# Norms of q and k through a 0/1 matrix, row-wise block transposes, and another rank for the local part

## The chip, the cores and the metric

The kernel runs on one core of one Trainium2 chip. The metric is device time in microseconds (us) of one execution; lower is better. An instruction belongs to one engine and each engine runs its own list in order: TensorE (PE) multiplies matrices, VectorE (DVE) and ScalarE (ACT) do elementwise work, GpSimd (POOL) does some of it too, and SyncE (SP) only issues DMA transfers. An instruction that waits for another engine or a transfer holds up everything behind it in its own list.

## The reference

One layer of a hybrid encoder, for a prompt of 2048 tokens and a sample of 32 tokens with a carried state:

```python
h = rmsnorm(x) * (1 + sc1) + sh1
p = h @ w_in                        # columns for u, v, q, k, vv, z, a, b
u, v = split(gelu(p_uv)); v = rmsnorm(v)
a_out = u * (W_s v + b_s)           # spatial gating over 128 positions
q, k, vv = silu(causal_conv(qkv))   # width 4
q = q * rsqrt(sum(q*q) + EPS) * 128 ** -0.5      # per token and head
k = k * rsqrt(sum(k*k) + EPS)
o, S = gated_delta_rule(q, k, vv, beta, g, S0)   # chunked, 4 heads of 128
b_out = rmsnorm(o) * silu(z)
x = x + gate1 * (concat(a_out, b_out) @ w_out)
h = rmsnorm(x) * (1 + sc2) + sh2
x = x + gate2 * (relu(h @ w_up) ** 2 @ w_down)
y = rmsnorm(x)
```

What matters here is the squared norm of every token's q and k in each head (a sum over 128 channels), and the transposed k and v, with tokens as rows, that the delta rule reads.

## The kernel before

Activations lie with channels on the 128 partitions and tokens along the row. Fp32 products of the large GEMMs are made from a high and a low half of each operand: `BH`/`BL` are the halves of the activations, `wh`/`wl` those of a weight slab. ACT writes the high half (a copy into a rounding type), DVE the low half (a subtraction); this is the "split" of a slab or of an activation, and a slab is split in two parts of 1024 columns. The program goes in stages: a startup (conditioning, z columns), the mixers in two halves of 1024 and 1056 tokens (the second with the sample), the output projection, the feed-forward part in three blocks of tokens.

In a half, `qkv_tile` makes one tile of q, k or v of one head, in two or three groups of 512, 384 or 288 tokens: 24 matmuls into a PSUM bank `g`, eviction by ACT into `raw`, the convolution by ACT and three DVE operations into `y`, SiLU into the row `yo`. Then one DVE instruction (`transpose32`) transposes the 32 x 32 blocks of `yo` into `yt`; k and v go from there to DRAM (`kt_d`) in four transfers. For k and q the tile `yt` is squared in place and summed over the 32 channels that each row now holds (`sums`, into `part`), and the four partial sums per token go to DRAM (`ns_d`).

`delta_local` is the delta rule's part that has no recurrence: it loads the decays (`dm`), loads the partial norms back, transposes them by a PE product with the identity (bank `B`), adds up the four parts, takes the reciprocal root, and then, for each of four batches of two chunks of 128 tokens, loads q and k from DRAM (`kq_d` into the ring `kq1`), multiplies k by (k, q) into bank `L` and evicts this by DVE. `delta_inv` inverts the triangular blocks of a pair of heads, a ladder of small PE products in bank `B` with DVE steps between them (block transposes `tr()` among them). `delta_chain` is the recurrence over chunks (bank `C`), `delta_out` its output, and `sample` all of this for the 32 sample tokens.

No order is written by hand. Every helper records an operation with an engine, an estimated cost and one of the ranks `CHAIN, INV, LOCAL, EVAC, GEMM, IDLE` (0 to 5). `schedule` then plays through the program with the estimated costs: at each moment the engine that is free takes the ready operation with the smallest key, and the order so found is the order of the instructions. Large GEMM products have rank GEMM, the local part LOCAL, and everything with no rank of its own EVAC: evictions, the splits, the convolution, the transposes, and the DMA loads for them. DMA issues are ordered in the same way, in the one queue of SP. A PE product that becomes ready early is thus fitted between GEMM products; how long things really take changes nothing in the order.

Of the kernel before, what the change touches and what calls it, by code (L numbers as in the profile page):

```python
# [17 lines left out]
P = 128  # L18
# [10 lines left out]
T0 = [0, 1024]  # L29
TW = [1024, 1056]  # L30
CHUNKS = [list(range(0, 8)), list(range(8, 17))]
WZ = 260
# [167 lines left out]
def R(x):  # L200
    return x.ap if isinstance(x, View) else x
# [11 lines left out]
class Program:  # L213
# [40 lines left out]
    def schedule(self):  # L254
# [91 lines left out]
class Kern:  # L346
# [57 lines left out]
    def transpose32(self, out, in_):  # L404
        nc = self.nc
        self.p.op(DVE, 68 + 1.042 * out.n, lambda: nc.vector.transpose(R(out), R(in_)), [out], [in_])

# [151 lines left out]
    def setup(self):  # L559
# [30 lines left out]
        rg("sp", [(6, 0)], (P, 3, 256))  # L590
        rg("ssl", [(6, 512), (6, 640)], (P, P))
# [39 lines left out]
        for n, s in (("convw", (P, 12, 4)), ("sconv", (P, 12, 3)), ("halo", (P, 12, 3)), ("cvo", (P, 2, 12, 3)),  # L631
                     ("ab", (P, 2, NC_, H)), ("ssv", (P, 2, NC_)), ("rq", (P, H, NC_)), ("ck", (P, H, NC_)),
                     ("dngc", (P, 1)), ("dtb", (P, H)), ("alog", (P, H)), ("nea", (P, H)), ("cs", (P, KT, 2)),
                     ("craw", (P, KT, 2)), ("gp", (P, H * 9)), ("gr", (P, P))):
            small(n, s, 17)
# [13 lines left out]
        self.kt_d = [[dt(f"kt_d{h}_{f}", [SLOT, 2, P]) for f in range(2)] for h in range(H)]  # L649
        self.ns_d = [[dt(f"ns_d{h}_{f}", [2, 4, SLOT]) for f in range(2)] for h in range(H)]  # L650
        self.z_d = [dt(f"z_d{h}", [P, T]) for h in range(H)]
# [138 lines left out]
    def consts(self, after):  # L790
# [4 lines left out]
        with self.p.at(GEMM):  # L795
# [11 lines left out]
            for h in range(H):  # L807
                fill(self.S[h], 0.0)
            fill(self.halo, 0.0)
            fill(self.yo[:, TW[0] :], 0.0)  # L810
            fill(self.ab, 0.0)
# [345 lines left out]
    def qkv_tile(self, hf, name, wh, wl, m):  # L1157
# [3 lines left out]
        for g, (o, w) in enumerate(GROUPS[hf]):  # L1161
# [18 lines left out]
            if ty < 2:  # L1180
                self.dma(self.kq_d[h][:, 1 - ty, T0[hf] + o : T0[hf] + o + w], yo)
        self.transpose32(self.yt.re("p (c j) -> p c j", j=32), self.yo.re("p (i c) -> p c i", i=32))
        if ty:
            for b in range(4):
                self.dma(self.kt_d[h][hf][:, ty - 1, 32 * b : 32 * b + 32].re("(i c) j -> i c j", i=32), self.yt[32 * b : 32 * b + 32].re("p (c j) -> p c j", j=32), 2 * P * SLOT)
# [14 lines left out]
    def delta(self, hf, h):  # L1200
        nb = self.new("nb")
        with self.p.at(LOCAL):
            self.delta_local(hf, h, nb)
# [6 lines left out]
    def delta_local(self, hf, h, nb):  # L1210

# [132 lines left out]
    def sample(self):  # L1344
# [7 lines left out]
        kg, vn, r1, oq, of = pk[:, 0, :P], pk[:, 1, :P], pk[:, 2, :P], pk[:, 0, P:], pk[:, 1, P:]  # L1352
        ns = self.new("ssl")[:, :8]
# [3 lines left out]
        ss, rr, ck, nk, rq, so, f, t1 = (sm[:, 8 + 2 * e : 10 + 2 * e] for e in range(8))  # L1357
        ck, nk, rq, so, f, t1 = (x[:, 0:1] for x in (ck, nk, rq, so, f, t1))
# [4 lines left out]
        with self.p.at(LOCAL):  # L1363
            for e, v in enumerate((self.beta, self.gc, self.egc, self.ekg)):
                self.cp(cols[:, :, e], v[:NS, :, c])
            for h in range(H):
                self.dma(kqs[:, :, own[h]], self.kq_d[h][:, :, t0 : t0 + NS])
                for e, v in enumerate((kg, vn)):
                    self.dma(v[own[h]], self.kt_d[h][1][TW[0] :, e])
                self.dma(ns[own[h]], self.ns_d[h][1][:, :, TW[0] :].re("x b t -> t (x b)"))  # L1370
                self.dma(sm[own[h], 0:4], cols[:, h])
# [8 lines left out]
            self.act(n32, n32, AF.Exp)  # L1380
            self.sums(ss, ns.re("p (x b) -> p x b", x=2))
            self.act(kg, kg, AF.Copy, scale=ekg)
            self.ts(ss, ss, EPS, ALU.add)
            self.rsqrt_small(rr, ss)
# [695 lines left out]
```

## Time and profile before

| | us |
|---|---|
| three runs | 2316.13, 2319.79, 2321.12 (median 2319.79) |
| profiled execution | 2325.33 |
| its span, first to last instruction | 2323.6 |
| PE busy in the span | 2276.7 (98%) |
| DVE busy | 1704.0 (73%) |
| ACT busy | 1197.5 (52%) |
| POOL busy | 554.9 (24%) |
| mean granted TensorE clock | 0.993 |

The names in the profile are those of tiles: `s` is any of the kernel's SBUF slots, `g`, `L`, `B`, `C`, `M` and `f` are PSUM banks by their use. Since helpers record the operations, a line number says only the kind: L422 is a matmul, L433 a PE transpose, L360 an ACT operation, L375, L380 and L389 are DVE (or POOL) elementwise operations, L406 the block transpose, L1194 a sum, L413 a DMA. Where PE is nearly always busy, what counts is the time in which it is not, and the time in which it runs at a lower clock: the view of what PE waited for and the clock of each stretch tell both.

### The profile page before, as it was taken

What the parts mean: (1) busy time and instruction counts of PE and PEld (TensorE: products, weight loads), DVE (VectorE), ACT (ScalarE), POOL (GpSimd) and SP (SyncE); (2) the same over time, 40 slices, a digit from 0 to 9 for tenths busy, and PEclk for the clock granted to TensorE, in tenths of its full rate; (3) what the DMA queues carried; (4) which work ended last, traced back from release to release, by engine and by line L of the source; (5) the groups of instructions that cost most, each with busy time, mean ns of one, the idle gap of its engine ahead of it and who ended that gap; (6) DMA issues with size and microseconds to landing.
All of it is one profiled execution on the core that took longest, in us unless ns stands there. A gap on an engine that the chain in (4) does not pass through costs nothing.

```text
span 2323.6 us, 44705 instructions
## 1 busy us (share of the span) xinstructions
PE 2276.7 (98%) x15703; PEld 2159.8 (93%) x15703; DVE 1704.0 (73%) x3528; ACT 1197.5 (52%) x2547; POOL 554.9 (24%) x699
## 2 busy tenths in 40 slices
PE   9999989999999999999999999999999999999998
PEld 6877768999999888999999999999999999999998
DVE  6558766688864546589999989877668886666775
ACT  5465445665544544466555555754344564334344
POOL 1214341312312223345445433200000250000001
PEclk9999999999999999999999999999999999999999
DMA  8578876666756767887677787997668797766761
GB/s 316 167 272 246 214 203 216 179 187 180 185 151 193 247 196 233 255 289 269 237 262 257 248 273 243 342 318 246 222 214 258 258 297 241 222 214 217 250 220 54
DMA packets 431793, 539.69 MB, mean 232 GB/s; under 512 B 137528, under 2 KB 264908, under 8 KB 431568
## 3 DMA queue, kind: packets, MB, share of 16 engines
q1 hardware_dynamic: 431568, 536.83, 72.7%
q8 instruction: 124, 2.03, 0.4%
q14 instruction: 101, 0.83, 0.1%
HBM read 387.10 MB, written 149.58 MB: 231 GB/s over the span
## 4 chain that ended last, share of the span: by engine, by line
PE 51%; DVE 2%; issue 1%; POOL 1%; ACT 1%; DMA 0%; SPq 0%; POOLq 0%; DVEq 0%; ACTq 0%
PE f L422 51%; DVE s L375 1%; POOL s L375 1%; ACT s L360 1%; DVE wl L375 1%; DMA s<-w_u 0%; DVE s L380 0%; DMA s<-x_d 0%; ACT wh L360 0%; PE M L422 0%; PE M L433 0%; SPq L413 0%; DVE BL L375 0%; POOL wr L375 0%; ACT BH L360 0%
## 5 line engine op out<-in xcount | busy, mean ns | idle before, releaser
L360 ACT ACTIVATE s<-s 128x348 f32<-128x348 f32 (+13 forms) x1075 | 505.9, 495 | 335.7 <-DVE s L375 152.0
L422 PE MATMUL f<-s,wh 128*128 128x348 f32 (+1 forms) x2768 | 662.4, 322 | 1.9 <-ACT s L360 1.3
L422 PEld LDWEIGHTS f<-s,wh 128*128 128x128 f32 x2768 | 480.6, 188 | 3.8 <-ACT s L360 1.9
L375 DVE TENSOR_TENSOR s<-f,s 128x348 f32<-128x348 f32 (+1 forms) x696 | 347.5, 512 | 172.9 <-PE f L422 171.4
L422 PE MATMUL f<-s,wl 128*128 128x348 f32 (+1 forms) x1384 | 444.7, 321 | 0.0
L422 PE MATMUL g<-BH,wh 128*128 128x384 f32 (+2 forms) x1104 | 409.1, 371 | 4.5 <-ACT BH L360 3.6
L422 PE MATMUL g<-BH,wl 128*128 128x384 f32 (+2 forms) x1104 | 390.3, 354 | 2.0 <-DVE wl L375 2.0
L422 PE MATMUL g<-BL,wh 128*128 128x384 f32 (+2 forms) x1104 | 391.0, 354 | 0.6 <-DVE BL L380 0.5
L375 DVE TENSOR_TENSOR s<-s,s 128x348 fp32r<-128x348 f32 (+9 forms) x650 | 350.8, 569 | 48.9 <-ACT s L360 23.0
L422 PE MATMUL f<-BH,wh 128*128 128x348 f32 (+1 forms) x1024 | 330.0, 322 | 0.7 <-DVE s L375 0.7
L422 PE MATMUL f<-BL,wh 128*128 128x348 f32 (+1 forms) x1024 | 329.2, 321 | 0.0
L375 POOL TENSOR_TENSOR s<-s,s 128x512 f32<-128x512 f32 (+18 forms) x303 | 244.2, 810 | 355.1 <-ACT s L360 168.6
L422 PE MATMUL f<-BH,wl 128*128 128x348 f32 (+1 forms) x1024 | 328.9, 321 | 0.0
L360 ACT ACTIVATE wh<-s 128x512 fp32r<-128x512 f32 x282 | 176.3, 632 | 227.7 <-PE f L422 181.6
L422 PEld LDWEIGHTS f<-s,wl 128*128 128x128 f32 x1384 | 260.5, 188 | 0.0
L375 DVE TENSOR_TENSOR wl<-s,wh 128x512 fp32r<-128x512 f32 x282 | 215.0, 769 | 38.1 <-ACT wh L360 37.8
L422 PEld LDWEIGHTS g<-BH,wh 128*128 128x128 f32 x1104 | 209.9, 190 | 31.4 <-issue 6.7
L422 PEld LDWEIGHTS g<-BH,wl 128*128 128x128 f32 x1104 | 209.9, 190 | 22.3 <-DVE wl L375 2.4
L422 PEld LDWEIGHTS g<-BL,wh 128*128 128x128 f32 x1104 | 209.9, 190 | 17.8 <-DVE BL L380 0.8
L360 ACT ACTIVATE wh<-wr 128x512 fp32r<-128x512 f32 (+2 forms) x159 | 124.1, 781 | 135.3 <-PE f L422 58.3
L422 PEld LDWEIGHTS f<-BH,wh 128*128 128x128 f32 x1024 | 192.4, 188 | 1.2 <-ACT wh L360 1.0
L422 PEld LDWEIGHTS f<-BH,wl 128*128 128x128 f32 x1024 | 193.0, 188 | 0.0
(130 smaller groups left out, 3141.0 us busy)
## 6 DMA issues: line engine op xcount, KB each, us to landing
s<-w_u SPq DMA_DIRECT2D x124, 256.0 KB, 3.2
s<-w_d SPq DMA_DIRECT2D x121, 256.0 KB, 4.4
wh<-su_d SPq DMA_DIRECT2D x114, 256.0 KB, 3.7
wl<-su_d SPq DMA_DIRECT2D x114, 256.0 KB, 4.0
wh<-sd_d SPq DMA_DIRECT2D x100, 256.0 KB, 3.4
wl<-sd_d SPq DMA_DIRECT2D x100, 256.0 KB, 3.4
wr<-w_b SPq DMA_DIRECT2D x36, 512.0 KB, 3.9
s<-adaw SPq DMA_DIRECT2D x32, 512.0 KB, 6.7
```

Of the source, the lines that this page charges most:

```text
L360: self.p.op(ACT, c, lambda: nc.scalar.activation(out=R(out), in_=R(in_), func=func, **{k: R(v) for k, v in kw.items()}), [out, accum], [in ...
L375: self.p.op(eng, c, lambda: e.tensor_tensor(out=R(out), in0=R(a), in1=R(b), op=op), [out], [a, b])
L422: nc.tensor.matmul(R(out), R(l), R(r), **kw)
```

## The change

1. `transpose32` of a q, k or v tile reads the row as it stands: block c is tokens 32c to 32c + 31, where before it was every 33rd token. The first half transposes 1024 columns and not 1056, and the estimate for this operation goes from 1.042 to 1.1 ns a column. The transfers to `kt_d` write the matching rows.
2. The squares go into slot 19 (whose halves are the ring `y` of the convolution), in two pieces in the first half and one in the second, and no longer over `yt`. The sums of k and q lie side by side in one tile `part`.
3. The way of the norms over DRAM is gone: 16 stores to `ns_d`, 8 loads and 4 small loads for the sample. `delta_local` multiplies `part` by a 0/1 matrix `same` (128 x 128, with a one where two partitions agree modulo 32), which leaves the sum over the four channel blocks in every partition; four DVE operations (five in the second half, one of them for the sample) pick the columns from PSUM and add EPS.
4. For all engines but PE, and for the DMA queue, the ranks LOCAL and EVAC are exchanged.

```diff
+        turn = {LOCAL: EVAC, EVAC: LOCAL}
-        key = [(o.prio, due[i] if o.prio >= EVAC else i, i) for i, o in enumerate(ops)]
+        key = [(o.prio if o.eng == PE else turn.get(o.prio, o.prio), due[i] if o.prio >= EVAC else i, i) for i, o in enumerate(ops)]
...
-        self.p.op(DVE, 68 + 1.042 * out.n, lambda: nc.vector.transpose(R(out), R(in_)), [out], [in_])
+        self.p.op(DVE, 68 + 1.1 * out.n, lambda: nc.vector.transpose(R(out), R(in_)), [out], [in_])
...
-        rg("ssr", [(14, 256), (14, 288)], (P, 32))
-        rg("sqp", [(4, 896), (4, 932)], (P, 33))
+        rg("ssr", [(6, 512), (6, 544)], (P, 32))
+        rg("sqp", [(4, 896), (4, 962)], (P, 2, 33))
+        self.same = self.slot(14, 256, (P, P))
...
-        self.transpose32(self.yt.re("p (c j) -> p c j", j=32), self.yo.re("p (i c) -> p c i", i=32))
+        nb = TW[hf] // 32
+        yt = self.yt[:, : TW[hf]]
+        self.transpose32(yt, self.yo[:, : TW[hf]])
...
-            self.act(self.yt, self.yt, AF.Square)
-            part = self.new("sqp")
-            self.sums(part, self.yt.re("p (c j) -> p c j", j=32))
-            self.dma(self.ns_d[h][hf][1 - ty].re("b (i c) -> (b i) c", i=32), part)
+            for c0, c1 in PIECES[hf]:
+                sq = self.slot(19, HALF if c0 else 0, (P, 32 * c1 - 32 * c0))
+                self.act(sq, yt[:, 32 * c0 : 32 * c1], AF.Square)
+                self.sums(self.part[:, 1 - ty, c0:c1], sq.re("p (c j) -> p c j", j=32))
...
-        ns, rr = self.new("ssl"), self.new("ssr")
-        self.dma(ns[:64], self.ns_d[h][hf][:, :, :TW[0]].re("x b (c p) -> (x b) c p", p=P))
+        rr = self.new("ssr")
         ss, rr = rr[:, :16], rr[:, 16:]
         pt = self.bank("B")
-        self.tr(pt[:, :64], ns[:64], self.ident[:64, :64])
-        self.sums(ss.re("p (x c) -> p x c", x=2), pt[:, :64].re("p (x b c) -> p x c b", x=2, b=4))
-        self.ts(ss, ss, EPS, ALU.add)
+        self.mm(pt[:, :66], self.same, part.re("p x c -> p (x c)"))
+        pv = pt[:, :66].re("p (x c) -> p x c", x=2)
+        for q in range(4):
+            d = slice(32 * q, 32 * q + 32)
+            self.ts(ss[d].re("p (x c) -> p x c", x=2), pv[d, :, q:32:4], EPS, ALU.add)
+            if hf == 1 and q == h:
+                self.ts(self.sss[d], pv[d, :, 32], EPS, ALU.add)
```

In the rows below, a name ends in the number of its buffer; a row with `x4` is four equal instructions that follow each other. Line numbers of the changed kernel are two higher.

On PE, at the output projection of the second half, before. `C<-ident` is the transpose of the sample's result in `sample`, and `g ... 128x288` the first products on the last 288 tokens, which hold the sample; `BH_71` to `BH_78` are the eight input tiles, the last four of which come from the delta rule:

```order
L422 MATMUL g_10058<-BH_78,wl 128x384
L422 MATMUL g_10127<-BH_71,wh 128x288
L422 MATMUL g_10127<-BL_79,wh 128x288
L422 MATMUL g_10127<-BH_71,wl 128x288
L422 MATMUL g_10127<-BH_72,wh 128x288
L422 MATMUL g_10127<-BL_80,wh 128x288
L422 MATMUL g_10127<-BH_72,wl 128x288
L433 MATMUL C_10171<-ident,s_481 128x128
L422 MATMUL g_10127<-BH_73,wh 128x288
```

And now:

```order
L424 MATMUL g_9964<-BH_75,wh 128x384
L424 MATMUL g_9964<-BL_83,wh 128x384
L424 MATMUL g_9964<-BH_75,wl 128x384
L424 MATMUL M_10036<-ones,s_491 128x1 x4
L435 MATMUL C_10032<-ident,s_473 128x128
L424 MATMUL g_9964<-BH_76,wh 128x384
```

The transpose of the sample stood six products behind the first one on 288 tokens; it now stands 58 large products ahead of it.

On DVE, at the end of the first half's convolutions, before. `wl` is the low half of a slab part (the last two of this half), `s_494<-s_493` the convolution, and the rows with 288, 256 and 32 columns belong to the normalised input of the second half:

```order
L375 TENSOR_TENSOR wl<-wr_96,wh 128x1024
L1194 TENSOR_REDUCE s_479<-s_483 128x33
L380 SCALAR_TENSOR_TENSOR s_494<-s_493,s_492,s_494 128x512
L406 STREAM_TRANSPOSE s_483<-s_495 128x1056
L380 SCALAR_TENSOR_TENSOR s_494<-s_493,s_492,s_494 128x512
L375 TENSOR_TENSOR s_497<-s_497,s_486 128x288 x2
L389 TENSOR_SCALAR s_497<-s_497,a_89,modc 128x256
L389 TENSOR_SCALAR s_497<-s_497,a_89,modc 128x32
L375 TENSOR_TENSOR s_496<-s_496,s_486 128x288
L375 TENSOR_TENSOR wl<-wr_96,wh 128x1024
```

And now (the first of the two `wl` stands ahead of this, with one small operation between):

```order
L382 SCALAR_TENSOR_TENSOR s_486<-s_485,s_484,s_486 128x512 x4
L408 STREAM_TRANSPOSE s_475<-s_487 128x1024
L382 SCALAR_TENSOR_TENSOR s_486<-s_485,s_484,s_486 128x512
L377 TENSOR_TENSOR s_489<-s_489,s_478 128x288 x2
L391 TENSOR_SCALAR s_489<-s_489,a_89,modc 128x256
L391 TENSOR_SCALAR s_489<-s_489,a_89,modc 128x32
L391 TENSOR_SCALAR s_488<-s_488,a_89,modc 128x256
L391 TENSOR_SCALAR s_488<-s_488,a_89,modc 128x32
L377 TENSOR_TENSOR s_488<-s_488,s_478 128x288
L408 STREAM_TRANSPOSE s_470<-s_476 128x512
L377 TENSOR_TENSOR wl<-wr_96,wh 128x1024
```

Between the two parts of the slab now stand five convolution steps where there were two, one sum less, the first step of the inverse (the transpose of 512 columns), and two operations more for the second half's input.

On DVE, at the first ladder of the inverse (`s_478<-B` and `s_484<-B`, later `s_470<-B` and `s_476<-B`, are its steps on PSUM), before. `s_493`, `s_494` and `s_495` with 512 columns are the spatial gate's products, which read a transfer from `s_d`:

```order
L406 STREAM_TRANSPOSE s_478<-s_484 128x512
L389 TENSOR_SCALAR s_478<-B_2711 128x8x16
L389 TENSOR_SCALAR s_478<-B_3438 128x8x16
L375 TENSOR_TENSOR s_494<-s_494 128x512
L375 TENSOR_TENSOR BL_79<-s_497,BH_71 128x384
L375 TENSOR_TENSOR s_484<-B_3482,s_484 128x8x16
```

And now:

```order
L391 TENSOR_SCALAR s_470<-B_2471 128x8x16
L382 SCALAR_TENSOR_TENSOR s_486<-s_485,s_484,s_486 128x512
L391 TENSOR_SCALAR s_470<-B_3323 128x8x16
L408 STREAM_TRANSPOSE s_475<-s_487 128x1024
L377 TENSOR_TENSOR s_489<-s_489,s_478 128x288
L377 TENSOR_TENSOR s_476<-B_3370,s_476 128x8x16
```

Behind the second step the ladder's third stood after a product on a transfer from `s_d` and a split; it now stands after a tile's block transpose and a product on a transfer of x.

On PE the product that brings the norms of head 0 in the first half stands, by a count of the rows, 60 large products behind the last one of its q tile (before: 183), that of head 1 stands 72 behind (before: 192).

More of the change, by code (lines that the diff above doesn't have):

```diff
@@ L30 @@
 TW = [1024, 1056]
+PIECES = [[(0, 16), (16, 32)], [(0, 33)]]
 CHUNKS = [list(range(0, 8)), list(range(8, 17))]
@@ L649, in setup @@
         self.kt_d = [[dt(f"kt_d{h}_{f}", [SLOT, 2, P]) for f in range(2)] for h in range(H)]
-        self.ns_d = [[dt(f"ns_d{h}_{f}", [2, 4, SLOT]) for f in range(2)] for h in range(H)]
         self.z_d = [dt(f"z_d{h}", [P, T]) for h in range(H)]
@@ L808, in consts @@
                 fill(self.S[h], 0.0)
+            d = self.ident.re("p (s r) -> p s r", s=4)
+            sm = self.same.re("p (s r) -> p s r", s=4)
+            self.tt(sm[:, 0], d[:, 0], d[:, 1], ALU.add)
+            for e in (2, 3):
+                self.tt(sm[:, 0], sm[:, 0], d[:, e], ALU.add)
+            for e in (1, 2, 3):
+                self.cp(sm[:, e], sm[:, 0])
             fill(self.halo, 0.0)
-            fill(self.yo[:, TW[0] :], 0.0)
             fill(self.ab, 0.0)
@@ L1181, in qkv_tile @@
                 self.dma(self.kq_d[h][:, 1 - ty, T0[hf] + o : T0[hf] + o + w], yo)
-        self.transpose32(self.yt.re("p (c j) -> p c j", j=32), self.yo.re("p (i c) -> p c i", i=32))
+        nb = TW[hf] // 32
+        yt = self.yt[:, : TW[hf]]
+        self.transpose32(yt, self.yo[:, : TW[hf]])
         if ty:
             for b in range(4):
-                self.dma(self.kt_d[h][hf][:, ty - 1, 32 * b : 32 * b + 32].re("(i c) j -> i c j", i=32), self.yt[32 * b : 32 * b + 32].re("p (c j) -> p c j", j=32), 2 * P * SLOT)
+                d = slice(32 * b, 32 * b + 32)
+                self.dma(self.kt_d[h][hf][: TW[hf], ty - 1, d].re("(c i) j -> i c j", i=32), yt[d].re("p (c j) -> p c j", j=32), 2 * P * TW[hf])
+        if ty == 1:
+            self.part = self.new("sqp")
         if ty < 2:
-            self.act(self.yt, self.yt, AF.Square)
-            part = self.new("sqp")
-            self.sums(part, self.yt.re("p (c j) -> p c j", j=32))
-            self.dma(self.ns_d[h][hf][1 - ty].re("b (i c) -> (b i) c", i=32), part)
+            for c0, c1 in PIECES[hf]:
+                sq = self.slot(19, HALF if c0 else 0, (P, 32 * c1 - 32 * c0))
+                self.act(sq, yt[:, 32 * c0 : 32 * c1], AF.Square)
+                self.sums(self.part[:, 1 - ty, c0:c1], sq.re("p (c j) -> p c j", j=32))
     def sums(self, out, in_):
@@ L1202, in delta @@
         with self.p.at(LOCAL):
-            self.delta_local(hf, h, nb)
+            self.delta_local(hf, h, nb, self.part)
         self.nbs.append(nb)
@@ L1208, in delta, with delta_local @@
             self.nbs = []
-    def delta_local(self, hf, h, nb):
+    def delta_local(self, hf, h, nb, part):
         c0 = CHUNKS[hf][0]
@@ L1356, in sample @@
         beta, gc, egc, ekg, negc = (sm[:, e : e + 1] for e in range(5))
-        ss, rr, ck, nk, rq, so, f, t1 = (sm[:, 8 + 2 * e : 10 + 2 * e] for e in range(8))
+        ss = self.sss
+        rr, ck, nk, rq, so, f, t1 = (sm[:, 8 + 2 * e : 10 + 2 * e] for e in range(7))
         ck, nk, rq, so, f, t1 = (x[:, 0:1] for x in (ck, nk, rq, so, f, t1))
@@ L1369, in sample @@
                     self.dma(v[own[h]], self.kt_d[h][1][TW[0] :, e])
-                self.dma(ns[own[h]], self.ns_d[h][1][:, :, TW[0] :].re("x b t -> t (x b)"))
                 self.dma(sm[own[h], 0:4], cols[:, h])
```

6 lines of the change are left out of this document (1 added, 5 removed).

## The prediction

> **What bounds the kernel.** I read the head of the page first, then busy time by stage, then what PE waited for, then the clock.
>
> ```profile
> span 2323.6 us, 44705 instructions
> PE 2276.7 (98%) x15703; PEld 2159.8 (93%) x15703; DVE 1704.0 (73%) x3528; ACT 1197.5 (52%) x2547; POOL 554.9 (24%) x699
> ```
>
> PE is busy for 2276.7 of 2323.6 us. The change takes no large product away, so all that it can win is in the 46.9 us in which PE stands, and in what a lower clock costs. The stages (first number after the stretch: its length, second: PE busy; then PE loads, DVE, ACT, POOL, the granted clock, DMA share and rate) say where this is:
>
> ```profile
> 20.00:250.00 230.00, 230.00 (x1433) 180.59 (x1433) 161.52 (x314) 125.89 (x224) 63.56 (x83) 1.00 0.74 241
> 250.00:360.00 110.00, 95.84 (x637) 75.36 (x636) 72.22 (x107) 54.30 (x97) 34.40 (x65) 0.95 0.81 218
> 360.00:700.00 340.00, 333.05 (x3169) 319.05 (x3167) 253.59 (x705) 193.87 (x469) 81.75 (x204) 0.99 0.65 181
> 700.00:800.00 100.00, 93.60 (x995) 88.49 (x994) 53.53 (x158) 49.66 (x135) 25.86 (x68) 1.00 0.70 203
> 800.00:1050.00 250.00, 246.67 (x1453) 226.59 (x1453) 152.00 (x312) 123.01 (x279) 85.60 (x74) 0.99 0.76 249
> 1100.00:2310.00 1210.00, 1209.06 (x7609) 1207.04 (x7608) 950.05 (x1829) 609.48 (x1262) 235.85 (x183) 1.00 0.74 243
> ```
>
> The first stretch has no gap, and the feed-forward part from 1100 on has 0.9 us in 1210. The mixers from 250 to 1050 have 14.2 + 7.0 + 6.4 + 3.3 = 30.9 us of idle PE. This is the change's ground. The view of PE's waits, between 250 and 1050 (total us, times, longest):
>
> ```profile
> PE L L422 <- DMA s<-kq_d: 4.6, 6, 1.6
> PE B L422 <- DVE s L406: 4.1, 4, 2.4
> PE B L422 <- DVE s L375: 3.5, 1, 3.5
> PE L L422 <- issue: 3.4, 3, 1.6
> PE C L422 <- ACT s L360: 2.5, 2, 1.7
> PE g L422 <- DVE wl L375: 2.0, 1, 2.0
> PE g L422 <- ACT BH L360: 1.7, 1, 1.7
> PE B L422 <- DVE s L389: 1.5, 2, 1.0
> PE g L422 <- ACT s L360: 0.9, 1, 0.9
> ```
>
> No single cause carries it: the local products (bank L) wait for loads of q and k, the ladder of the inverse (bank B) for DVE, the large products (bank g) for a split or an eviction. The clock adds to it (after the five busy columns stands the granted clock):
>
> ```profile
> 323.00:327.00 4.00, 4.00 (x12) 3.15 (x11) 2.12 (x4) 3.94 (x6) 3.74 (x9) 0.57 0.84 245
> 350.00:358.00 8.00, 6.47 (x78) 5.28 (x79) 4.04 (x7) 7.00 (x14) 0.00 (x0) 0.57 0.94 291
> 937.00:942.00 5.00, 5.00 (x25) 4.87 (x26) 3.56 (x8) 1.99 (x5) 1.01 (x1) 0.66 0.91 261
> ```
>
> Each of these stretches follows one of these waits of PE (start, us, and in brackets the wait before it):
>
> ```profile
> 319.52 0.40 PE L422 MATMUL g<-BH,wh 128*128 128x512 f32 x1
> 319.75 0.39 PE L422 MATMUL g<-BL,wh 128*128 128x512 f32 x1
> 322.16 0.50 PE L422 MATMUL g<-BH,wl 128*128 128x512 f32 x1 [2.01 <-DVE wl L375]
> ...
> 351.53 1.05 PE L422 MATMUL B<-s,s 32*32 32x16 f32 x64 [3.50 <-DVE s L375]
> ...
> 936.44 0.40 PE L422 MATMUL g<-BH,wh 128*128 128x288 f32 x1 [1.65 <-ACT BH L360]
> ```
>
> So a wait of 1.7 to 3.5 us is followed by some us at half clock, and costs about twice its length. The Trainium skill (TensorE: Matmul & The Clock Gate, Part 1) says that the clock falls after at least one idle window of about 3.4 us and that the windows run free of the program; the trace disagrees on the length, since 2.01 and 1.65 us were enough here.
>
> **The change, part by part.** *Block transposes and sums.* The groups of operations (count, busy us, mean ns):
>
> ```profile
> L380 DVE SCALAR_TENSOR_TENSOR s<-s,s,s 128x512 f32<-128x512 f32 x72 | 60.3, 860 | 12.8 <-ACT s L360 11.9 <-POOL s L398 0.3
> L406 DVE STREAM_TRANSPOSE s<-s 128x1056 f32<-128x1056 f32 x24 | 51.9, 2164 | 4.4 <-ACT s L360 2.7 <-DMA kt_d<-s 1.4
> L1194 DVE TENSOR_REDUCE s<-s 128x33 f32<-128x1056 f32 x16 | 20.0, 1248 | 5.0 <-ACT s L360 4.9
> L406 DVE STREAM_TRANSPOSE s<-s 128x512 f32<-128x512 f32 x8 | 5.7, 707 | 4.2 <-DMA s<-ud_d 4.1
> L389 DVE TENSOR_SCALAR s<-s 128x8 f32<-128x8 f32 x16 | 2.6, 195 | 0.0
> ...
> L360 ACT ACTIVATE s<-s 128x512 f32<-128x512 f32 x56 | 34.2, 624 | 39.5 <-DVE s L406 18.2 <-DVE s L380 8.9 <-DMA kq_d<-s 6.7
> ```
>
> The strided transpose takes 2164 ns for 1056 columns, which is 2.05 ns a column; the one of 512 columns, which reads its row as it stands, 1.38. At that rate a new one takes at most 1.41 us (1024) or 1.46 (1056), so the 24 give back about 24 x 0.73 = 17.5 us of DVE. The schedule believed in 1.17 us and now believes in 1.19 to 1.23: where it was 1.0 us wrong at every tile, it is 0.2 wrong. Against this stand the 8 sums that become two each (the row of 1248 ns: at most 0.15 us more apiece, 1.2 in all, if a piece costs little above its share) and 36 small operations on PSUM for 16 small ones that go (20 x 0.195 = 3.9 us). Net about 12 us of DVE, none of it on PE by itself. The two squares of the first half cost ACT 2 x 0.62 for one instruction; ACT stands half of the time.
>
> *The norms' way.* PE loses eight transposes and gets eight products of 66 columns:
>
> ```profile
> L433 PE MATMUL B<-ident,s 64*128 64x64 f32 x8 | 2.2, 272 | 0.0
> L422 PE MATMUL L<-s 128*128 128x256 f32 x128 | 34.4, 387 | 7.9 <-DMA s<-kq_d 4.1 <-issue 3.4 <-PE C L422 0.3
> ```
>
> The new product lies between these rows (0.27 and 0.39), nearer the first by its size, so 0 to +0.9 us in all; I take 0. It waits for DVE's last sum with large products queued behind it. Its cover is 60 products for head 0, at 0.23 us from start to start (319.52 to 319.75) 13.8 us. What must be done in it: eviction, first tap and SiLU on ACT (3 x 0.62), three taps (3 x 0.86), transpose 1.41, the last square 0.62 and sum 0.7, 7.2 us. So 6.6 us remain for queues on DVE, and I cost it at nothing. On SP 28 transfers go:
>
> ```profile
> L413 SPq DMA_DIRECT2D ns_d<-s x16: 319/327/940, 197.1 to 646.5; - x16
> L413 SPq DMA_DIRECT2D s<-ns_d x12: 422/636/807, 213.1 to 681.3; - x12
> L413 SPq DMA_DIRECT2D kt_d<-s x64: 561/742/3817, 182.2 to 663.3; - x64
> ```
>
> By the medians 16 x 0.33 + 12 x 0.64 = 13 us of its queue. But the stores to `kt_d`, up to 3.8 us each at the head of that queue, stay, and the loads for bank L stand behind them. Of the 8.0 us of waits in bank L (4.6 + 3.4) I take off 1.0; the ends are 8.0 off, and 20 more (second rival). The setup of `same` (seven small DVE operations) lies in a stage in which PE has no gap; if it delayed PE it would cost 7 x 0.2 = 1.4 us.
>
> *The ranks.* They move DVE, ACT and SP work. The three places of the order shown above:
>
> (a) The wait of 1.65 us before the 128x288 product: the sample's transpose now stands 58 large products earlier, about 10 us (this stage has 1453 PE instructions in 246.67 us, 0.17 us each). Wait and clock, 1.65 + 5 x 0.34 = 3.4 us, go whole. If the sample is late by more than those 10 us, it is 0.
>
> (b) The wait of 2.01 us for `wl`, and (c) the ladder's 2.4 (longest of L406) and 3.50:
>
> ```profile
> 316.27 2.19 DVE L406 STREAM_TRANSPOSE s<-s 128x1056 f32<-128x1056 f32 x1
> 320.89 1.21 DVE L375 TENSOR_TENSOR wl<-wr,wh 128x1024 fp32r<-128x1024 f32 x1
> ...
> 347.84 0.69 DVE L375 TENSOR_TENSOR s<-s 128x512 f32<-128x512 f32 x1 [3.29 <-DMA s<-s_d]
> 351.19 0.28 DVE L375 TENSOR_TENSOR s<-B,s 128x128 f32<-128x128 f32 x1
> ```
>
> In (b) the slow transpose stands ahead of the split. It becomes 0.8 us shorter, but by the order shown three more taps (0.86 each) are now between the slab's parts. Worth 2.0 + 4 x 0.43 = 3.7 with the clock; I take half, 1.9. In (c) DVE stood 3.29 us for a transfer, with the ladder's step behind it. Now another product on a transfer stands ahead of that step, so half again: 2.4 + 3.5 + 8 x 0.43 less the 0.8 that the low clock cost while PE stood anyway is 8.5; I take 4.3. Both have the ends 0 and all.
>
> *The other ladders:* the rest of L406 and L389 (1.7 + 1.5), half of it for the shorter transposes: 1.6. *The feed-forward part:* the output stores rank below weight loads now; its 0.9 us of gaps bound a gain, and the stores are few, 0.
>
> *New waits.* The order of PE changes nearly everywhere between 250 and 1050, and the waits listed above are of about 1 us each. I put three new ones against the gain: 3.0.
>
> Sum: 1.9 + 4.3 + 3.4 + 1.0 + 1.6 - 3.0 = 9.2 us. The profiled execution took 2325.33 us, 1.7 more than its span and 5.5 more than the median of the runs, 2319.79. Less 9.2 this is 2316.1 on its scale, and 2310.6 on that of the median, which I predict. If the waits of (a) and (b) cost no half clock, 1.7 and 0.9 go from the sum: 2313.2.
>
> **Rivals.** *The waits only move.* For it: most of them end on a transfer or on DVE behind a transfer, and neither the stores to `kt_d` nor the latency changes; the order is still made from costs that are too low (0.86 us for a tap). Against it: (a). About 2319.8.
>
> *Slower: the local loads starve.* The loads of q and k for bank L and the evictions of L now rank behind all slab loads, splits and evictions. There are 32 such batches; nine waited, 8.0 us, 0.89 each. If all do, this is 28.5, 20.5 more than now, and with the 9.2 the time is 2331. It decides from 19 waiting batches on ((8.0 + 9.2) / 0.89). Against it: the order of PE was made with the same ranks, so the products moved along.
>
> *Slower: the squares block the convolution.* They share slot 19 with `y`, in the second half all of it, so the next tile's first tap waits for the sum. If this holds an eviction at each of the 16 k and q tiles, at the 0.9 us of the row of g behind ACT, it costs 14.4, and the time is 2325. It decides from 10 tiles on. Against it: three banks and two `raw` rows lie between.
>
> *The half clock stays:* if the low stretches at 323 and 937 are not the work of the waits of 2.01 and 1.65 us ahead of them, they stay when these go, and the time is 2313.2. Against it: each begins within 1.3 us of its wait's end. It is what the rule of the Trainium skill (TensorE: Matmul & The Clock Gate, Part 1) would give for waits this short.
>
> **Numbers.** Forecast 0.61, half clock stays 0.05, waits only move 0.18, starving loads 0.11, blocked convolution 0.05. A run of this kernel tells 0.2% (4.6 us) from no change: faster 0.66, same 0.18, slower 0.16. The low end, 2297, has (a), (b), (c) and the ladders whole and half of bank L's waits: 3.4 + 3.7 + 8.5 + 3.2 + 4.0 = 22.8. The high end, 2325, takes in the blocked convolution and leaves out the starving loads.
>
> **What would show it.** The 24 block transposes at 1.2 to 1.5 us; no wait of PE for BH near 935 and no clock below 1 after it; fewer or shorter waits of g for `wl` and of B for DVE between 300 and 360; waits of L for `kq_d` of about 7 us; PE idle in the mixers near 24 instead of 31 us. I am wrong if DMA landing makes as many waits at other places, if L waits at most batches, or if a wait of over 2 us appears at the new product.

## The result, and the profile after

| | before | after |
|---|---|---|
| median of 5 runs, us (range) | 2319.79 (2315.25 to 2321.20) | 2300.53 (2297.68 to 2305.96) |
| profiled execution, us | 2325.33 | 2299.66 |

The ratio of the times is 0.9928, with a 95% interval of 0.9907 to 0.9948. The change takes 19.3 us off the median, against a forecast of 9.2: the direction is right, the time lies within the range, and the size is about twice what the prediction summed up.

The head of the page of the changed kernel:

```profile
span 2297.9 us, 44731 instructions
PE 2264.7 (99%) x15711; PEld 2154.3 (94%) x15711; DVE 1685.6 (73%) x3560; ACT 1206.3 (52%) x2560; POOL 557.6 (24%) x698
```

PE now stands for 33.2 us of its span, where it stood for 46.9. Its busy time is 12.0 us lower too, although it does the same large products: a lower clock had stretched some of them, by some 8.6 us in the stretches that are added up further down; the rest of the 12.0 is not placed. The stages of the changed kernel, and behind them a stretch after one wait and the three that had run at a low clock (columns as in the prediction: length, PE busy, PE loads, DVE, ACT, POOL, granted clock, DMA share and rate):

```profile
20.00:250.00 230.00, 228.88 (x1428) 180.77 (x1427) 156.76 (x340) 133.84 (x238) 63.12 (x83) 1.00 0.78 250
250.00:360.00 110.00, 105.93 (x886) 85.22 (x884) 79.56 (x140) 61.36 (x108) 38.72 (x67) 1.00 0.86 242
360.00:700.00 340.00, 332.81 (x3046) 322.10 (x3045) 240.70 (x717) 193.71 (x482) 84.68 (x204) 0.99 0.64 178
700.00:800.00 100.00, 97.33 (x999) 89.99 (x998) 54.83 (x150) 49.66 (x128) 25.39 (x69) 1.00 0.75 228
800.00:1050.00 250.00, 248.03 (x1486) 231.79 (x1486) 165.58 (x317) 133.12 (x296) 98.59 (x80) 1.00 0.78 254
1050.00:1100.00 50.00, 48.49 (x303) 47.95 (x302) 47.98 (x80) 29.86 (x61) 25.93 (x17) 1.00 0.75 255
1100.00:2285.00 1185.00, 1183.43 (x7449) 1181.37 (x7448) 926.30 (x1787) 594.63 (x1233) 220.13 (x174) 1.00 0.74 243
277.00:285.00 8.00, 5.62 (x25) 4.33 (x24) 4.40 (x7) 6.42 (x13) 5.10 (x17) 1.00 0.95 274
323.00:327.00 4.00, 4.00 (x38) 3.02 (x39) 2.36 (x5) 3.90 (x9) 0.23 (x1) 1.00 0.99 205
350.00:358.00 8.00, 8.00 (x47) 6.95 (x46) 6.06 (x17) 4.16 (x8) 2.44 (x1) 1.00 0.99 356
442.00:446.00 4.00, 3.27 (x24) 2.78 (x24) 1.16 (x3) 2.26 (x5) 0.00 (x0) 0.57 0.18 55
937.00:942.00 5.00, 5.00 (x31) 5.00 (x30) 2.84 (x5) 3.13 (x5) 2.11 (x3) 1.00 1.00 350
```

Length less PE busy gives the idle time of each stage: 1.1 + 4.1 + 7.2 + 2.7 + 2.0 = 17.0 us from 20 to 1050, where it was 30.9. Most of the fall, 14.2 to 4.1, lies between 250 and 360, where the clock is whole as well. What is left of a low clock between 20 us and the last 10 us is one stretch at 442. (The changed kernel runs ahead, by 27 us at the end of the mixers, so equal times are not equal work in the two kernels; but it has no low clock at another place either.) The feed-forward part is no faster: its gaps grew a little (1.6 us from 1100 on, 0.9 before).

The view of what PE waited for, between 250 and 1050 (total us, times, longest), shows which waits have gone and which have come:

```profile
PE C L424 <- DVE s L382: 4.4, 7, 1.2
PE L L424 <- DMA s<-kq_d: 2.9, 2, 2.4
PE B L424 <- issue: 2.0, 1, 2.0
PE L L424 <- DVE s L382: 1.9, 1, 1.9
PE B L424 <- DVE s L377: 1.6, 1, 1.6
PE f L424 <- ACT s L362: 1.4, 1, 1.4
PE C L435 <- DVE s L391: 0.9, 1, 0.9
PE f L424 <- DVE s L377: 0.5, 2, 0.3
```

By bank, against the whole list of before (with its small rows, which the prediction left out): `g` 4.6 us to none, those for `wl` and `BH` among them, `B` 10.7 to 3.6, `L` 8.3 to 4.8, `M` 1.3 to none. The recurrence (`C`) waits more, 5.3 us against 4.0, and `f` 1.9 against 1.6.

The groups of operations of the changed kernel that answer to those shown of before (count, busy us, mean ns, idle before):

```profile
L382 DVE SCALAR_TENSOR_TENSOR s<-s,s,s 128x512 f32<-128x512 f32 x72 | 55.6, 799 | 13.4 <-ACT s L362 9.9 <-POOL s L400 2.9
...
L408 DVE STREAM_TRANSPOSE s<-s 128x1056 f32<-128x1056 f32 x12 | 15.3, 1275 | 2.6 <-ACT s L362 2.5
L408 DVE STREAM_TRANSPOSE s<-s 128x1024 f32<-128x1024 f32 x12 | 14.9, 1241 | 7.6 <-ACT s L362 4.6 <-DMA kt_d<-s 3.1
L1206 DVE TENSOR_REDUCE s<-s 128x16 f32<-128x512 f32 x16 | 10.4, 680 | 4.1 <-ACT s L362 4.1
L1206 DVE TENSOR_REDUCE s<-s 128x33 f32<-128x1056 f32 x8 | 10.0, 1250 | 4.2 <-ACT s L362 4.2
L424 PE MATMUL B<-s,s 128*128 128x66 f32 x16 | 2.6, 247 | 0.0
```

The 24 block transposes take 30.2 us together where they took 51.9. The last row is the new product of the norms (two records to a product): it costs 2.6 us in all and PE never waited ahead of it.

### The profile page after: what moved, and what is told of

It is laid out like the page before. It is cut to its first block, busy times and chain, and to the rows that moved or that the text cites. A ratio compares the mean times of both kernels' runs of the same rounds, so it can differ in the third digit from the quotient of the medians.

```text
span 2297.9 us, 44731 instructions
## 1 busy us (share of the span) xinstructions
PE 2264.7 (99%) x15711; PEld 2154.3 (94%) x15711; DVE 1685.6 (73%) x3560; ACT 1206.3 (52%) x2560; POOL 557.6 (24%) x698
## 4 chain that ended last, share of the span: by engine, by line
PE 84%; DVE 5%; DMA 5%; ACT 3%; issue 2%; POOL 1%; SPq 1%; POOLq 0%; DVEq 0%; ACTq 0%
PE f L424 51%; PE g L424 25%; PE C L424 3%; PE B L424 2%; ACT s L362 2%; DVE s L377 2%; DVE s L382 1%; PE L L424 1%; DVE wl L377 1%; PE M L424 1%; DMA wr<-w_b 1%; SPq L415 1%; DMA s<-xT 1%; POOL s L377 1%; DMA s<-kt_d 1%
## 5 line engine op out<-in xcount | busy, mean ns | idle before, releaser
L362 ACT ACTIVATE s<-s 128x348 fp32r<-128x348 f32 (+14 forms) x1083 | 506.1, 493 | 310.1 <-DVE s L377 137.1
L377 DVE TENSOR_TENSOR s<-s,s 128x348 fp32r<-128x348 f32 (+8 forms) x651 | 350.0, 567 | 40.4 <-ACT s L362 18.4
```

The source lines that it names most:

```text
L362: self.p.op(ACT, c, lambda: nc.scalar.activation(out=R(out), in_=R(in_), func=func, **{k: R(v) for k, v in kw.items()}), [out, accum], [in ...
L377: self.p.op(eng, c, lambda: e.tensor_tensor(out=R(out), in0=R(a), in1=R(b), op=op), [out], [a, b])
```

## Experiments

All runs, with the idle time of PE from 20 to 1050 us, taken from the stages of each profile as above. "Before" is the kernel before, timed in the same rounds.

| run | median us (range) | before | ratio, 95% interval | PE idle, mixers |
|---|---|---|---|---|
| before / after | 2319.79 / 2300.53 | | 0.9928, 0.9907 to 0.9948 | 30.9 / 17.0 |
| e1_ranks_alone | 2321.60 (2317.19 to 2324.01) | 2319.04 | 1.0009, 1.0000 to 1.0018 | 29.9 |
| e2_data_path_alone | 2314.99 (2312.77 to 2321.82) | 2319.04 | 0.9986, 0.9976 to 0.9996 | 27.9 |
| e5_slow_transposes_after | 2309.20 (2303.10 to 2311.77) | 2319.04 | 0.9955, 0.9942 to 0.9968 | 20.4 |
| e6_fast_transposes_before | 2313.57 (2307.05 to 2321.06) | 2319.04 | 0.9974, 0.9963 to 0.9985 | 19.0 |
| l_before | 2320.96 (2316.52 to 2325.98) | 2319.30 | 1.0007, 0.9997 to 1.0016 | 31.7 |
| l_ranks_alone | 2323.11 (2317.78 to 2328.93) | 2319.30 | 1.0018, 1.0007 to 1.0030 | 28.7 |
| l_data_path_alone | 2315.54 (2312.64 to 2320.79) | 2319.30 | 0.9984, 0.9974 to 0.9993 | 26.5 |
| l_after | 2303.93 (2298.23 to 2306.95) | 2319.30 | 0.9929, 0.9915 to 0.9943 | 18.3 |
| m1_dma_ranks_only | 2322.01 (2314.58 to 2325.52) | 2318.97 | 1.0007, 0.9994 to 1.0020 | 31.0 |
| m2_engine_ranks_only | 2307.29 (2301.59 to 2311.16) | 2318.97 | 0.9940, 0.9921 to 0.9958 | 20.6 |
| b1_output_stores | 2302.55 (2298.97 to 2303.43) | 2318.97 | 0.9921, 0.9905 to 0.9937 | 20.8 |
| b2_store_cost | 2301.24 (2299.42 to 2306.38) | 2318.97 | 0.9919, 0.9900 to 0.9938 | 20.4 |

The last column is one execution's, and idle time alone does not order the times: e6 has 19.0 us of it and b1 20.8, yet e6 is 11.0 us slower by the medians. In the profile of e6 the clock is low in three stretches (0.66 over 5 us from 272, 0.57 over 8 us from 334, 0.66 over 5 us from 726), which is about 6.8 us lost; the changed kernel has one of 1.7.

### The two parts of the change, each alone

The ranks alone, in the kernel before:

```diff
-        key = [(o.prio, due[i] if o.prio >= EVAC else i, i) for i, o in enumerate(ops)]
+        turn = {LOCAL: EVAC, EVAC: LOCAL}
+        key = [(o.prio if o.eng == PE else turn.get(o.prio, o.prio), due[i] if o.prio >= EVAC else i, i) for i, o in enumerate(ops)]
```

> The kernel before with the exchange of the ranks alone; block transposes (2.16 us) and the norms' way over DRAM stay. If the order by rank makes the gain, most of the 19 us is here: 2300 to 2306 us. If late DVE work (a transpose that takes 1.0 us more than the schedule believes) makes the waits, little is: 2313 to 2320, since the slow transposes still sit in DVE's list. If order luck decides, either way and no link to the ranks, within 2308 to 2326.

The data path alone (transposes in a row, squares in slot 19, norms by the product) is the changed kernel with that edit undone:

> The changed kernel with the ranks as before: row-wise transposes (1.24 us), norms by the 0/1 product, 28 transfers fewer. If late DVE work makes the waits, most of the gain is here: 2300 to 2307. If the ranks do, 2313 to 2320. The wait for BH near 935 stays if the ranks alone moved the sample's transpose forward, and goes if the data path did.

The ranks alone gain nothing (0 to 0.2% slower) and the data path alone gains about 4 us; together they gain 19. Neither run reached the 2300 to 2307 us that it was given if its part made the gain. So the parts need each other. Three of PE's waits with the ranks alone, between 250 and 1050:

```profile
PE g L423 <- DVE s L381: 4.3, 3, 2.8
PE B L423 <- DVE s L407: 3.9, 1, 3.9
PE g L423 <- ACT BH L361: 2.7, 1, 2.7
```

The ladder's wait of 3.9 us is for a transpose of its own, of 512 columns (start, us, in brackets the idle time before and what ended it):

```profile
335.12 0.73 PE L423 MATMUL B<-s,s 32*32 32x16 f32 x64 [3.91 <-DVE s L407]
```

What that transpose reads is a load from `ud_d`, which SP issues at 329.5; no transfer to or from `ud_d` lands in less than 3.6 us in this run, so it could not start before 333.1; DVE starts it at 334.4, behind two more splits. No tile's block transpose stands in this chain. At 929.6 the products on the sample's tokens wait for their `BH` again, longer than in the kernel before (2.7 us, there 1.65): on ACT two operations on the feed-forward part's input stand ahead of it, the first of which has waited 2.43 us for POOL. A lower clock follows, as this stretch shows:

```profile
930.00:937.00 7.00, 4.52 (x18) 3.86 (x19) 4.17 (x9) 3.32 (x7) 1.19 (x2) 0.76 0.91 294
```

With the data path alone both are cured (no wait of `g` for `BH` above 0.9 us, of `B` for a transpose 0.9), and another wait takes their place. The first row of the view of what PE waited for:

```profile
PE g L423 <- ACT s L361: 10.9, 6, 6.7
```

The longest of these in the timeline, on DVE, then ACT, then PE (start, us, in brackets the idle time before and what ended it):

```profile
263.37 1.25 DVE L407 STREAM_TRANSPOSE s<-s 128x1024 f32<-128x1024 f32 x1 [3.54 <-DMA kt_d<-s]
...
264.65 1.16 ACT L361 ACTIVATE s<-s 128x512 f32<-128x512 f32 x2 [4.07 <-DVE s L407]
...
270.87 2.28 ACT L361 ACTIVATE s<-s,s 128x128 f32<-128x128 f32 x7 [1.25 <-DMA s<-kt_d]
273.06 0.58 ACT L361 ACTIVATE s<-g 128x512 f32<-128x512 f32 x1
...
273.69 0.79 PE L423 MATMUL g<-BH,wh 128*128 128x512 f32 x1 [6.70 <-ACT s L361]
```

A tile's block transpose waits for the stores to `kt_d` that still read the row `yt`; ACT waits for the transpose, then does seven operations of the local part that wait for a load from `kt_d`; only then comes the eviction of `g`, for which PE stands 6.7 us. This is near to the prediction's third rival (work on a tile's row that holds an eviction), but through the stores and ACT's order and not through slot 19.

### Is it the luck of an order?

The planned latency of a transfer is raised by 2%, which changes the order and no work. Played through without the chip, the two schedules of the kernel before differ in the place of 183 of DVE's 3528 operations and 53 of PE's 4560; the exchange of the ranks alone moves 863 and 404. It was done to the kernel before, to each part alone and to the changed kernel:

```diff
-LAND, RATE = 3000, 140
+LAND, RATE = 3060, 140
```

> The kernel before with the schedule's estimate of a transfer's landing at 3060 and not 3000 ns, which says nothing new of the chip and only shuffles the order. It measures how much of any difference is luck of the order. If order luck is small against 19 us: 2316 to 2323. If it is large: anywhere from 2305 to 2330.

> Ranks exchanged alone, with the landing at 3060 ns. If the ranks by themselves give nothing: 2316 to 2326, as with 3000 (2321.6). If that was luck of the order: as low as 2305.

> Data path alone (old ranks), with the landing at 3060 ns. If its one wait of 6.7 us of g for an eviction, behind a transpose that waits for the stores to kt_d, is a property of the old ranks with the new data path: again 2312 to 2320 with long waits of g for ACT. If it was luck of the order: 2300 to 2308 and no such wait.

> The changed kernel with the landing at 3060 ns. If the two parts need each other: again 2297 to 2306, at least 8 us below the three others of this group. If 2300.5 was luck of the order: 2306 to 2318.

All four come out within 3.4 us of their unshuffled versions, in the same order of times. The waits come again at the same places: with the ranks alone 3.7 us of `B` behind a transpose and 2.4 us for `BH`; with the data path alone 6.1 us of `g` for ACT. So the pattern does not hang on one exact order, and a difference of 3 us between two orders says nothing. This is one shuffle, and smaller than the change itself: what a shuffle as large as the change would do by luck was not measured.

### How much of it is the speed of the transpose?

The changed kernel's order, in which every tile's transpose does 704 columns a second time, of which the schedule knows nothing:

```diff
+            nc.vector.transpose(R(out), R(in_))
+            if again:
+                nc.vector.transpose(R(out[:, :again]), R(in_[:, :again]))
...
-        self.transpose32(yt, self.yo[:, : TW[hf]])
+        self.transpose32(yt, self.yo[:, : TW[hf]], 704)
```

> The changed kernel with its order, but each of the 24 tile transposes does 704 of its columns a second time (about 0.9 us more on DVE that the schedule doesn't know of, as before). If late DVE work makes the waits: 8 us or more slower than the changed kernel, 2308 to 2316, with waits of B and g for DVE back. If the order makes the gain: 2300 to 2304.

The other way round, the order of before exactly, in which the transposes read their row as it stands (the rows of `yt` then hold other tokens):

```diff
-        self.transpose32(self.yt.re("p (c j) -> p c j", j=32), self.yo.re("p (i c) -> p c i", i=32))
+        self.transpose32(self.yt, self.yo)
...
-        self.ts(ss, ss, EPS, ALU.add)
+        self.ts(ss, ss, 1.0e3, ALU.add)
```

> The kernel before, instruction for instruction in its order, but the transposes read their row as it stands, which takes about 0.9 us less each; the tokens then lie in another order than the stores assume, and the norms get 1000 added, so the values are not the reference's. If late DVE work makes the waits: 8 us or more faster than before, 2306 to 2312, with the waits of B for L406 near 339 and of g for wl near 320 gone. If the order makes the gain: 2316 to 2320.

The groups of e5 (the added piece) and of e6:

```profile
L411 DVE STREAM_TRANSPOSE s<-s 128x704 f32<-128x704 f32 x24 | 21.9, 911 | 0.8
```

```profile
L406 DVE STREAM_TRANSPOSE s<-s 128x1056 f32<-128x1056 f32 x24 | 30.6, 1273 | 4.4 <-ACT s L360 2.7 <-DMA kt_d<-s 1.4
```

Adding 21.9 us of DVE to the changed kernel costs about 6 us by the ratios (0.9955 against 0.9928, whose intervals just touch) and 8.7 by the medians; taking 21.3 us away from the kernel before gains 6 (3.5 to 8.6 by the interval), with no instruction moved. That is less than the 8 us or more that was expected of e6 if late work on DVE made all the waits, and more than the other theory gave it. About a third of the change, then, is a shorter instruction in 24 places, in an order that needs no change for it. In e6 the wait for `wl` is gone and those of `B` fall from 10.7 to 5.6 us, though one of 3.5 us for a transpose stays. The sample's wait shrinks too: in the order of before, PE's timeline has

```profile
919.55 0.40 PE L422 MATMUL g<-BH,wh 128*128 128x288 f32 x1 [0.72 <-ACT BH L360]
```

where it had 1.65, and the clock stays whole from 925 to 945.

e5 says one thing more. Its transposes cost DVE as much as those of before, and yet it is 10 us faster than the kernel before (0.9955), while the ranks alone gain nothing. So the slow transposes are not all that holds the ranks back. What else of the data path the ranks need (the norms by the product, the squares' place, the 28 transfers that are gone) was not run apart, and stays open.

### Whose ranks?

The changed kernel with the ranks exchanged only in the DMA queue, and only on ACT, DVE and POOL:

```diff
+        key = [(turn.get(o.prio, o.prio) if o.eng == DMA else o.prio, due[i] if o.prio >= EVAC else i, i) for i, o in enumerate(ops)]
```

> The new data path whole, with the ranks of the local part and of the evictions exchanged in the DMA queue alone (ACT, DVE and POOL keep the old ranks). Theory A: the data path alone loses its gain because the stores to kt_d and the loads for bank L stand so in the one DMA queue that a tile's next block transpose waits for them (3.5 us at 263) and the evictions of g behind it; then the rank of the queue is the cure: no wait of g for ACT above 2 us between 250 and 300, PE idle in the mixers (20 to 1060) at most 21 us, 2300 to 2307 us. Theory B: the engines' own ranks are what lets evictions and splits go ahead of the local part; then the wait of g for ACT stays in some form (6 us or more in all) and the time is 2312 to 2318.

```diff
+        key = [(o.prio if o.eng in (PE, DMA) else turn.get(o.prio, o.prio), due[i] if o.prio >= EVAC else i, i) for i, o in enumerate(ops)]
```

> The new data path whole, with the ranks exchanged on ACT, DVE and POOL alone (the DMA queue keeps the old ones). Theory A (the queue's rank is the cure): the wait of a block transpose for the stores to kt_d near 263 stays, with g waiting for ACT, PE idle in the mixers 24 us or more, 2312 to 2318 us. Theory B (the engines' ranks are): PE idle at most 21 us, 2300 to 2307 us.

Theory A falls, though both times lie a little above what Theory B gave them (2312 to 2318 and 2300 to 2307). With the queue alone the wait for ACT is not cured but grows; with the engines' ranks it is gone. The first of PE's waits in m1:

```profile
PE g L424 <- ACT s L362: 18.0, 13, 6.5
```

Its groups of operations, the block transposes of the first half:

```profile
L408 DVE STREAM_TRANSPOSE s<-s 128x1024 f32<-128x1024 f32 x12 | 14.9, 1244 | 12.8 <-DMA kt_d<-s 7.6 <-ACT s L362 5.2
```

In m2 the list of PE's waits has none of `g` for `ACT s` at all; its first entry is:

```profile
PE B L424 <- DVE s L391: 4.5, 5, 1.3
```

and its block transposes of the first half:

```profile
L408 DVE STREAM_TRANSPOSE s<-s 128x1024 f32<-128x1024 f32 x12 | 14.9, 1242 | 13.1 <-DMA kt_d<-s 8.2 <-ACT s L362 4.9
```

The transposes still wait 8.2 us for the stores to `kt_d` in m2, as they do in m1. PE does not notice, since the evictions of `g` keep coming: around such a wait they start on ACT at 247.1, 256.2, 261.5 and 269.9 in m2, where with the data path alone none starts between 251.0 and 273.1. They are not wholly free of the local part: the one at 256.2 still follows seven of its operations. With the queue's rank as well, this wait is 3.1 us in the changed kernel and 3.7 in l_after. Whether that is worth time is not settled: the medians of m2 and of the changed kernel lie 6.8 us apart, but the intervals of their ratios overlap (0.9921 to 0.9958 and 0.9907 to 0.9948).

### Two attempts at more

The feed-forward part's output stores, recorded at the rank that gives them their old place in the DMA queue; and, on top of that, the stores to `kt_d` counted at 1.1 us of that queue in the schedule:

```diff
-                with self.p.at(LOCAL):
+                with self.p.at(EVAC):
```

> The changed kernel, with the feed-forward part's output stores recorded so that they have the same place against the loads of weights in the DMA queue as they had before the change. Theory: the exchange of ranks put these stores behind loads, and that is why PE's waits in bank f rose from 2.5 to 5.0 us; then they fall to 3 us or less, and the time is 1 to 3 us below the changed kernel's (2297 to 2300). Rival: these waits move with any new order, and the time stays within 1 us of the changed kernel's.

```diff
-        self.p.op(DMA, max(500, x), ...
+        self.p.op(DMA, max(issue, x), ...
...
-                self.dma(self.kt_d[h][hf]..., 2 * P * TW[hf])
+                self.dma(self.kt_d[h][hf]..., 2 * P * TW[hf], 1100)
```

> The kernel with the output stores' place as before, and in addition the stores to kt_d counted by the schedule at 1.1 us of the queue's time each and not 0.5 (the trace: 0.32 to 3.9 us, median 0.58). Theory: the waits of bank L for kq_d (2.9 us after the change, 4.6 before) come of loads that the schedule believes earlier than they are; with the dearer stores they fall to 1.5 us or less, 2294 to 2298 us. Rival: the order that comes out is just another one, and the time lies within 4 us of the one with the stores' place alone, on either side, with the waits of L unchanged.

Neither theory is borne out. PE's waits in bank `f`, of b1:

```profile
PE f L424 <- DVE s L377: 1.7, 3, 1.1
PE f L424 <- DVE s L382: 1.6, 2, 0.9
PE f L424 <- ACT s L362: 1.4, 1, 1.4
```

and in bank `L`, of b2:

```profile
PE L L424 <- DMA s<-kq_d: 4.9, 2, 3.5
PE L L424 <- DVE s L382: 1.9, 1, 1.9
```

The `f` waits are 4.7 us in all, against 5.0 in the changed kernel and 3.2 before (the expectation says 2.5). Behind 1050, where the stores are, they are 2.0 us in b1 and 2.7 in b2, against 3.1 in the changed kernel, 4.0 in l_after and 1.6 before: the stores' place may make 1 us of them, but an order moves them as much, and the time did not fall. The `L` waits of b2 are 6.8 us and did not fall either (4.7 in b1). Both kernels equal the changed one within what a new order does by itself. No version tried beats the change.

## Why the prediction was right, and by how much it was off

*Direction and place.* The prediction looked for the gain in the mixers' waits and the half clock behind them, and there it is: PE idle from 20 to 1050 fell from 30.9 to 17.0 us, where it had forecast about 24. The first product of the feed-forward part starts 27.3 us earlier (1008.6 before, 981.3 after); behind it nothing was won.

*Transposes and sums.* Of DVE's 12 us less it became 18.4 (1704.0 to 1685.6). The mis-sized term is the rate: 1.38 ns a column, read from a row of 512, holds that instruction's fixed part (707 ns for 512 columns and 1241 for 1024 make, as an estimate, 170 ns fixed and 1.04 a column), and 1024 and 1056 columns took 1.21. The 24 gave back 21.7 us and not 17.5; the sums grew by 0.4; and the taps became shorter (860 to 799 ns, 4.7 us), which no step had. What failed was a step further on: "none of it on PE by itself". e6 shows that this alone gives 6 us, at waits for `wl`, the ladder and the sample that the prediction had put to the order.

*Norms.* Right: the product costs 0.4 us more than the transposes that it replaces (2.6 for 2.2), and PE never waits ahead of it.

*(a), the sample, 3.4 us.* The gain came whole in this pair of profiles: no wait for `BH` in the mixers, and no low clock behind it. The cause given was wrong. The prediction put it to the ranks; with the ranks alone the wait is 2.7 us, with the data path alone it is gone, and with shorter transposes in the old order it is 0.72.

*(b) and (c), `wl` and the ladder, taken at half (1.9 + 4.3) with 1.6 for other ladders.* They came whole and more in this pair. The waits of `B` and that for `wl` fell from 10.7 + 2.0 to 3.6 us; the clock of 12 us at 323 and 350 rose from 0.57 to 1.00 (5.2 us), and a new stretch of 4 us at 442 costs 1.7. That is 9.1 + 5.2 - 1.7 = 12.6, less what is counted twice where PE stood at a low clock, against 7.8. The halving stood on what the new order put between the split's parts; the taps were there, but not late.

*Bank L, 1.0 off 8.0.* It was 3.5; but b2 has 6.8 where the changed kernel has 4.8, so this term moves with any order.

*New waits, 3.0.* About right: `C` took 1.3 more, `f` 0.3, and a wait of 1.1 came before 250, 2.7 in all. Against them two small waits went that no step had, `M` for POOL (1.3) and `g` for ACT (0.9).

*Output stores, 0.* The feed-forward part lost about 1.4 us (gaps of 0.7 and 0.9 became 1.5 and 1.6 between 1050 and 1100 and behind). b1 leaves open whether the stores made part of it: in it these gaps are 1.2 and 1.0, and the time is no better.

What the sum missed in kind is that its terms do not add: by the prediction's lines the ranks carried 9.6 us (a, b and c). Alone they carry none: in e1 other waits come in the place of those that go. The rivals: "the waits only move" is nearly true of each part alone (29.9 and 27.9 us of idle time for 30.9) and false of both; the local loads did not starve; PE waits for no eviction behind the squares (no wait of `g` between 250 and 1050); the half clock went with its waits.

*The clock, and luck.* About 3.9 us of the 9.2 were clock (1.7 in (a), 0.9 in (b), 1.3 in (c)), taken from one execution whose mean clock was 0.993. Of the 75 executions of the kernel before that were timed with the runs above one has 0.993, and their average is 0.9956; the five of the changed kernel average 0.9962. By this (an estimate: 0.0006 of 2300 us) the clock is worth 1 to 2 us between ordinary executions, where it is 8.6 between the two profiled ones. So the clock terms were sized on an unlucky execution, and that they came whole is in good part luck. One stretch shows it plainly. From 16 to 20 us the kernel before ran at 0.57, behind a wait of 1.97 us, and the changed one at 1.00, behind 1.59; but e6, with exactly the order of before, waits 1.08 us there and has a clock of 1.00 too.

The balance of the two profiled executions: 13.9 us of idle time in the mixers and 0.7 in the first 20 us; 5.2 + 1.7 - 1.7 us of clock at the stretches above, 1.7 at one that the prediction had not listed (0.76 over 7 us from 464) and 1.7 from 16 to 20; less 1.4 in the feed-forward part. That is 21.8 of the 25.7 us by which they differ; no row shown here says where the other 4 are. The medians differ by only 19.3, mostly because the profiled execution of before was 5.5 us above its median.

## What to carry to other kernels

Before an instruction's rank or place is changed, look whether one slow form of it makes the queue late everywhere: here 0.9 us off each of 24 transposes was worth 6 us of an engine that did not run them, with not one instruction moved. Two parts of a change that look separate in the diff can be worth nothing, a little, and five times that together; time each alone before crediting either, and shuffle the order, counting what has moved, to learn what an order is worth by luck. A wait that ends on an eviction is read two steps back: what stood ahead of the eviction in its own queue, and what that was waiting for.

## What the runs showed of the hardware

The way in which a block transpose reads its row sets its price: 2164 ns for 1056 columns in steps of 33 elements, 1273 ns with the same columns read in a row (e6, the same order). The Trainium skill (SBUF — State Buffer, Door 1: The DMA port swizzle) says that SBUF has lines of 16 bytes, that consecutive accesses within a line run at full bandwidth, and that crossing to a new line costs; these two numbers agree, as a step of 33 fp32 elements meets a new line every time; no run here tells this from another price of a step.

A wait's length does not decide whether the clock falls. In PE's timeline of the changed kernel

```profile
280.14 1.10 PE L424 MATMUL L<-s 128*128 128x256 f32 x4 [2.38 <-DMA s<-kq_d]
...
442.73 0.39 PE L424 MATMUL B<-s,s 32*32 32x16 f32 x11 [1.97 <-issue]
```

the wait of 2.38 us is followed by a clock of 1.00 (277 to 285), and that of 1.97 by 0.57 (442 to 446). Nor does it take such a wait: in the kernel before

```profile
464.00:471.00 7.00, 6.96 (x161) 6.60 (x160) 3.47 (x12) 5.11 (x12) 0.37 (x2) 0.76 0.88 278
```

PE waits at most 0.34 us at a time between 400 and 480, and the low clock at 466 stands behind 2.9 us of small products (`C`, `B` and `M`, from 463.45). So the prediction's "a wait of 1.7 to 3.5 us is followed by some us at half clock" holds at its three places and is no rule. The Trainium skill (TensorE: Matmul & The Clock Gate, Part 1) has windows that run free of the program, which fits two waits of like length with different outcomes; its length of about 3.4 us of idle time is more than the 1.97 us that were enough here. It would also fit the times of the changed kernel: three runs from 2297.7 to 2300.5 at a mean clock of 0.997, two at 2305.7 and 2306.0 at 0.995. That these two met more low stretches was not seen, since only one execution was profiled.
